# A hybrid decoder layer on one core: Toeplitz blocks read from rows of lags, rotation tables made inside the setup's loop, and a delta-net state carried by two products per chunk

## The chip, the cores and the metric

The kernel runs on one NeuronCore of a Trainium2 chip. The metric is the time of one execution on the device in microseconds; of the kernel before there are three runs and one more run under the profiler. TensorE multiplies, VectorE, ScalarE and GpSimd do the elementwise work, and DMA queues (most of them issued by SyncE) move data. The profile calls these engines PE, DVE, ACT, POOL and SP, and PEld is TensorE's loading of weights.

## The reference

One inference step of one layer: 2048 new positions, and eight single new tokens (samples) with states of their own. All is in fp32.

```python
n = rmsnorm(x, norm1_g);  proj = n @ w_in
y_s5  = s5_mixer(proj[:512], ...)          # diagonal state space, 32 groups of 16 channels, 64 states
y_gdn = gdn_mixer(proj[512:], ...)         # gated delta rule, 4 heads of 128
x = x + concat(y_s5, y_gdn) @ w_out
x = x + conv_ffn(rmsnorm(x, norm2_g))      # 1024 -> 2*2816 -> 1024, causal conv of width 3

# s5, per group: h[t] = Abar*h[t-1] + Bbar*u[t] (64 complex states),  y[t] = Re(C*h[t]) + d*u[t]

# delta rule, per head and chunk, state s (128 x 128):
decay = exp(gc_i - gc_j);  L = strict(beta * k k^T * decay)
sol   = solve(I + L, [beta*v, beta*k*exp(gc)])          # gives u_c, w_c
v_new = u_c - w_c @ s
o     = (q*exp(gc)) @ s + (q k^T * decay) @ v_new
s     = s*exp(gc_last) + (k*exp(gc_last-gc))^T @ v_new
```

The kernel takes chunks of 128 positions for the delta rule and blocks of 8 and 16 positions for the S5 scan.

## The kernel before, in words

The 2048 positions are four quarters of 512 (q = 3, 2, 1, 0 in the first loop). The large fp32 products are taken as three products of rounded halves (L287 to L289, 2992 + 928 of each), and these are most of TensorE's work. TensorE runs its instructions in one order; that order comes from the order of the steps in the program and a scheduler which plays the program through in a model of time.

**Setup (to about 240 us).** A loop over the quarters loads and normalizes x. In its third round, s5_setup makes the S5 operators, each for 8 batches of 4 groups, and writes them to DRAM: E and E2 (GpSimd, L489, three operations of 128x512 each), F and F2 (VectorE, then transposes), T2 (L510, a 128x128 product of F and E per group) and T (L516 makes one block M of 16 columns per group, L521 shifts it into 8 block columns by products with a shifted identity). T and T2 are Toeplitz: they hold one 16x16 block per lag. When the loop over batches is done its pool is closed, and a new pool s5c holds the rotation powers u0 to u10 (u[k+1] = u[k] squared, from L530) and the table CSt of all 32 groups, doubled in length six times (cmul, L337 to L342: six operations of VectorE for each complex product), which goes to tabD. The delta net's pool g is opened on the same side of SBUF when s5_setup has returned. Steps "u" (s5_in) project the S5 inputs, "c" (gdn_cols, L801 to L830) makes the delta net's gates.

**Mixers (about 240 to 620 us).** A string of letters sets the order of the steps: F gdn_front of a head (projections, conv, transposes, decay matrix; kg and vt are read from PSUM by ScalarE, L890 and L891), I gdn_inverse (the inverse T of I + L: 32x32 blocks on VectorE from an identity X copied at L924, then products), B gdn_back (four chunks in turn, L977 to L989), b and h the two halves of s5_batch, one batch of groups. s5_batch loads F, F2, tab, T, T2, E and E2 of a batch, 13 tiles in a ring (NM).

**gdn_back, a chunk.** Two products of the state (L977, L978), rv on VectorE (L980: vt minus the first, scaled), T times rv (L982), vn on VectorE, then kg times vn and AT times vn (L986, L987), and VectorE adds the state (L988) and the output (L989).

**Feed-forward (620 us to the end).** A second string does the up and down projections in pieces (r, s), and between them F, I and B of the three further quarters (12 heads). A step I is put ahead of others by a high priority.

Of the kernel before, what the change touches and what calls it, by code (L numbers as in the profile page):

```python
# [9 lines left out]
F32 = mybir.dt.float32  # L10
# [13 lines left out]
NW, NWR, NV, NG, NM, UPB = 8, 2, 9, 4, 13, 1  # L24
# [18 lines left out]
MIXERS = ("FbbhbFhhIbBbIhbhbFBIFhIhbBhxB")  # L43
FFN = ("NFIrLrrSFrrrrrrBFIrBIrrrFIrrNBFrBIrrFrBrIrrFrrIBrrFrrIBrrrrNBrFIrFrrBFIrrrrIrBBrrrrrrrrrFr"
       "rrrIBrrrrGrrrsrsrrrrrrsrsrrrrrrrr")
# [57 lines left out]
def consts(c):  # L103
# [51 lines left out]
    c.Xi = cp.tile([128, 4, 32], F32, name="Xi")  # L155
    xi = c.V("xi", I32)[:, :128].rearrange("p (a b) -> p a b", a=4)
    nc.gpsimd.iota(xi, pattern=[[-1, 4], [1, 32]], base=1024, channel_multiplier=-4)
    nc.vector.tensor_scalar(xi, xi, 31, None, op0=OP.bitwise_and)
    nc.vector.tensor_scalar(c.Xi, xi, 0.0, None, op0=OP.is_equal)
# [185 lines left out]
def s5_setup(c):  # L345

    nc, tc, inp, ps = c.nc, c.tc, c.inp, c.ps
    c.TD, c.FD, c.ED, c.TD2, c.FD2, c.ED2 = (c.dram(n, 8, 128, 512) for n in ("TD", "FD", "ED", "TD2", "FD2", "ED2"))
# [4 lines left out]
    with ExitStack() as es:  # L353
# [4 lines left out]
        def small(name, n=32):  # L358
            return sp.tile([128, n], F32, name=name)
# [22 lines left out]
        kk = small("kk")  # L382
        nc.vector.tensor_scalar(kk, th, 1.0 / (2 * math.pi), 12582912.0, op0=OP.mult, op1=OP.add)
        nc.vector.tensor_scalar(kk, kk, 12582912.0, None, op0=OP.subtract)
        r = small("r")
# [3 lines left out]
        r2, sn, cs = small("r2"), *(keep.tile([128, 32], F32, name=n) for n in ("sn", "cs"))  # L389
# [9 lines left out]
        nc.vector.tensor_scalar(cs, cs, 1.0, None, op0=OP.add)  # L399

# [14 lines left out]
        p, den, t, fr, fi = (small(n) for n in ("p_", "den", "t_", "fr", "fi"))  # L415
# [47 lines left out]
        rev = lambda P, r: P[r, :, 15::-1]  # L463
# [9 lines left out]
        AD = sp.tile([128, 32, 16], F32, name="AD", tag="Bi")  # L473
        nc.vector.tensor_tensor(AD[96:128], dbc[96:128].rearrange("p (g c) -> p g c", c=16),
                                c.ident[96:128, None, 112:128].to_broadcast([32, 32, 16]), op=OP.mult)
        shift = sp.tile([128, 240], F32, name="shift")
        nc.vector.memset(shift[:, 128:240], 0.0)
        nc.vector.tensor_copy(shift[:, 0:128], c.ident)
        for b in range(8):
            gs = slice(4 * b, 4 * b + 4)  # L480
# [3 lines left out]
            def outer(eng, dst, x, xp, y, yp):  # L484

                t = sp.tile(sh, F32, name="ot", tag="cm" if eng is nc.vector else "op", bufs=2 if eng is nc.vector else 1)
                eng.tensor_tensor(dst, x[:, gs, None, :].to_broadcast(sh), xp[:, :, :, None].to_broadcast(sh), op=OP.mult)
                eng.tensor_tensor(t, y[:, gs, None, :].to_broadcast(sh), yp[:, :, :, None].to_broadcast(sh), op=OP.mult)
                eng.tensor_tensor(dst, dst, t, op=OP.add)  # L489
            for k, dram in ((1, c.ED), (9, c.ED2)):  # L490
                E = st("Et", 2)
                outer(nc.gpsimd, E, CrT, PA[:, gs, k:k + 8], CiT, PB[:, gs, k:k + 8])
                if k == 1:
                    E1 = E
                nc.sync.dma_start(dram[b], E.rearrange("p a b c -> p (a b c)"))
# [10 lines left out]
            M = sp.tile([128, 4, 16], F32, name="M", bufs=2)  # L506

            pt = ps("s")
            for g in range(4):
                nc.tensor.matmul(pt[:, g * 128:(g + 1) * 128], lhsT=FTf[:, g], rhs=E1[:, g].rearrange("p s c -> p (s c)"), start=True, stop=True)  # L510
            T2 = sp.tile([128, 512], F32, name="T2", tag="ev", bufs=2)
            nc.scalar.activation(T2, pt, AF.Copy)
            nc.sync.dma_start(c.TD2[b], T2)
            pm = ps("s")
# [4 lines left out]
            pT = ps("s")  # L519
            for j in range(8):  # L520
                nc.tensor.matmul(pT[:, j * 64:(j + 1) * 64], lhsT=shift[:, 16 * (7 - j):16 * (7 - j) + 128],  # L521
                                 rhs=M.rearrange("p g c -> p (g c)"), start=True, stop=True)
            To = sp.tile([128, 4, 8, 16], F32, name="Tt", tag="ev", bufs=2)
            nc.scalar.activation(To, pT.rearrange("p (j g c) -> p g j c", j=8, g=4), AF.Copy)
            nc.sync.dma_start(c.TD[b], To.rearrange("p a b c -> p (a b c)"))
        inner.close()
        sp = es.enter_context(tc.tile_pool(name="s5c", bufs=1, side="right"))

        u8 = [sp.tile([128, 2, 32], F32, name=f"u{k}") for k in range(11)]
        nc.vector.tensor_copy(u8[0][:, 0], cs)  # L530
        nc.vector.tensor_copy(u8[0][lo, 1], sn[lo])
        nc.vector.tensor_scalar(u8[0][hi_, 1], sn[hi_], -1.0, None, op0=OP.mult)

        def rot(outc, outs, ac, as_, bc, bs, shape):
            cmul(nc, sp, outc, outs, ac, as_, bc, bs, shape, "rot")
        for k in range(10):
            rot(u8[k + 1][:, 0], u8[k + 1][:, 1], u8[k][:, 0], u8[k][:, 1], u8[k][:, 0], u8[k][:, 1], [128, 32])
        CSt = sp.tile([128, 2, 32, 65], F32, name="CSt")
        Ct, St = CSt[:, 0], CSt[:, 1]
        nc.vector.memset(Ct[:, :, 0], 1.0)  # L540
        nc.vector.memset(St[:, :, 0], 0.0)
        for k in range(6):
            n = 1 << k
            m = min(32, 512 // n)
            for h in range(32 // m):
                hs = slice(m * h, m * h + m)
                b_ = lambda i: u8[4 + k][:, i, hs, None].to_broadcast([128, m, n])
                rot(Ct[:, hs, n:2 * n], St[:, hs, n:2 * n], Ct[:, hs, 0:n], St[:, hs, 0:n], b_(0), b_(1), [128, m, n])
        nc.vector.tensor_copy(Ct[:, :, 64], u8[10][:, 0])
        nc.vector.tensor_copy(St[:, :, 64], u8[10][:, 1])  # L550
        for k in range(8):
            nc.sync.dma_start(c.tabD[k].rearrange("p (a r) -> p a r", a=2), CSt[:, :, 4 * k:4 * k + 4].rearrange("p a g m -> p a (g m)"))


def s5_in(c, q, nT, pre, ws, rsB):

    nc = c.nc
    for t in range(4):
        rows = slice(t * 128, t * 128 + 128)
        up = pre.tile([128, QT], F32, name="up", bufs=UPB).rearrange("p (s r m) -> p s r m", s=8, r=2)  # L560
# [915 lines left out]
```

## Time and profile before

| | |
|---|---|
| median of three runs | 2806.24 us (2805.96, 2806.24, 2814.92) |
| profiled execution | 2812.43 us, of which the span of instructions is 2810.5 us |
| PE busy | 2683.3 us, 95% of the span |
| DVE, ACT, POOL busy | 2134.0, 1388.2, 694.9 us (76%, 49%, 25%) |
| chain that ended last | PE 76%, DVE 13%, DMA 5%, ACT 2%, issue 2%, SP's queue 1% |

The chain that ended last follows back, from the last instruction, what released each step; PE holds three quarters of it. Busy shares are means over stages that differ: the setup, the mixers and the feed-forward stage are told apart by reading the busy time in stretches of the span. The granted clock stands in the same rows as a share of 2.4 GHz, so 0.50 would be a stretch wholly at 1.2 GHz.

### The profile page before, as it was taken

The numbers are of one execution on the slowest core, as the hardware profiler recorded it, in microseconds if no ns is written. First come the engines' busy times: TensorE is split into PE (matmuls) and PEld (weight loads), VectorE is DVE, ScalarE is ACT, GpSimd is POOL, SyncE is SP. The second block draws the span as 40 slices with busy tenths as digits, with TensorE's granted clock in tenths as the row PEclk, the third lists the DMA queues.
The fourth block names the chain that finished last, engine by engine and source line by source line (L and its number), as shares of the span: only waits on it lengthen the run. The fifth ranks groups of instructions, "written<-read, shape, count | busy, mean of one in ns | idle before, by whom it ended". The sixth has DMA issues, their size and how long they took to land.

```text
span 2810.5 us, 43670 instructions
## 1 busy us (share of the span) xinstructions
PE 2683.3 (95%) x15568; PEld 2290.5 (81%) x15568; DVE 2134.0 (76%) x4642; ACT 1388.2 (49%) x2774; POOL 694.9 (25%) x972
## 2 busy tenths in 40 slices
PE   5998898999999999998999999999999998999998
PEld 4887887787988999998777878877888787788887
DVE  6867887866779879778598777986777877676776
ACT  3635555555555454444544554544545445544443
POOL 4636331100121212212331111213221122322223
PEclk9999998999999999999999999999999999999999
DMA  7756443435324233333434333344333334533432
GB/s 195 240 158 189 127 131 106 123 91 152 108 83 115 84 95 87 95 92 111 130 97 117 95 91 102 89 130 125 96 103 93 92 89 128 164 98 98 129 112 68
DMA packets 427308, 325.15 MB, mean 116 GB/s; under 512 B 75823, under 2 KB 372184, under 8 KB 427075
## 3 DMA queue, kind: packets, MB, share of 16 engines
q1 hardware_dynamic: 416755, 293.76, 36.0%
q0 software_dynamic: 10336, 28.61, 3.3%
q8 instruction: 122, 2.00, 0.3%
q14 instruction: 95, 0.78, 0.1%
HBM read 268.94 MB, written 53.63 MB: 115 GB/s over the span
## 4 chain that ended last, share of the span: by engine, by line
PE 76%; DVE 13%; DMA 5%; ACT 2%; issue 2%; SPq 1%; POOL 0%; DVEq 0%; POOLq 0%; ACTq 0%
PE psmm L287 17%; PE psmm L289 17%; PE psmm L288 17%; PE psd L287 5%; PE psd L288 5%; PE psd L289 5%; DVE wlo L73 1%; DVE tm L929 1%; DMA N<-nD 1%; DVE X L930 1%; DVE x L1125 1%; DMA mr<-mixT 1%; PE psf L905 1%; PE psf L869 1%; DVE t L846 1%
## 5 line engine op out<-in xcount | busy, mean ns | idle before, releaser
L287 PE MATMUL psmm<-nT,whi 128*128 128x512 f32 (+2 forms) x2992 | 1066.8, 358 | 18.1 <-ACT t L843 5.8
L288 PE MATMUL psmm<-nT,whi 128*128 128x512 f32 (+2 forms) x2992 | 1061.8, 355 | 2.8 <-DVE nT L73 1.4
L289 PE MATMUL psmm<-nT,wlo 128*128 128x512 f32 (+2 forms) x2992 | 1060.4, 355 | 0.0
L72 ACT ACTIVATE whi<-wr 128x1024 fp32r<-128x1024 f32 x372 | 393.8, 1060 | 576.8 <-PE psmm L288 419.5
L287 PEld LDWEIGHTS psmm<-nT,whi 128*128 128x128 f32 x2992 | 570.4, 191 | 98.7 <-ACT t L843 6.8
L288 PEld LDWEIGHTS psmm<-nT,whi 128*128 128x128 f32 x2992 | 571.2, 191 | 81.1 <-DVE nT L73 3.0
L289 PEld LDWEIGHTS psmm<-nT,wlo 128*128 128x128 f32 x2992 | 570.5, 191 | 78.0 <-issue 1.1
L73 DVE TENSOR_TENSOR wlo<-wr,whi 128x1024 fp32r<-128x1024 f32 x356 | 445.0, 1251 | 96.6 <-ACT whi L72 92.7
L1125 DVE TENSOR_TENSOR x<-psd,x 128x512 f32<-128x512 f32 (+2 forms) x464 | 257.2, 558 | 134.1 <-PE psd L289 132.1
L287 PE MATMUL psd<-gt,whi 128*128 128x512 f32 (+2 forms) x928 | 324.0, 349 | 16.8 <-DVE x L1125 14.7
L288 PE MATMUL psd<-gt,whi 128*128 128x512 f32 (+2 forms) x928 | 317.2, 342 | 0.0
L289 PE MATMUL psd<-gt,wlo 128*128 128x512 f32 (+2 forms) x928 | 315.6, 341 | 0.0
L1272 DVE SCALAR_TENSOR_TENSOR t<-raw,cc,t 128x512 f32<-128x512 f32 x352 | 275.8, 785 | 15.4 <-ACT t L1269 9.7
L1273 POOL COPY halo<-raw 128x2 f32<-128x2 f32 x176 | 79.2, 450 | 778.6 <-DVE raw L1268 709.8
L287 PEld LDWEIGHTS psd<-gt,whi 128*128 128x128 f32 x928 | 175.4, 189 | 47.7 <-DVE x L1125 22.3
L73 POOL TENSOR_TENSOR gt<-s,gt 128x512 fp32r<-128x512 f32 (+1 forms) x88 | 126.2, 1434 | 333.1 <-ACT gt L72 311.5
L288 PEld LDWEIGHTS psd<-gt,whi 128*128 128x128 f32 x928 | 175.6, 189 | 21.6
L289 PEld LDWEIGHTS psd<-gt,wlo 128*128 128x128 f32 x928 | 175.1, 189 | 20.9
L1268 DVE TENSOR_TENSOR raw<-psmm,rs 128x512 f32<-128x512 f32 (+1 forms) x214 | 123.9, 579 | 71.7 <-PE psmm L289 70.3
L1269 ACT ACTIVATE t<-raw,cc 128x512 f32<-128x512 f32 (+1 forms) x176 | 127.1, 723 | 69.3 <-DVE raw L1268 66.2
L929 DVE TENSOR_TENSOR tm<-X,N 128x124 f32<-128x124 f32 (+30 forms) x496 | 131.2, 265 | 39.0 <-DMA N<-nD 27.2
L1135 POOL TENSOR_TENSOR sq<-sq 128x256 f32<-128x256 f32 (+3 forms) x84 | 96.7, 1151 | 223.8 <-ACT sq L1133 221.3
(504 smaller groups left out, 3656.1 us busy)
## 6 DMA issues: line engine op xcount, KB each, us to landing
wr<-in_ffn_w_up_dram SPq DMA_DIRECT2D x176, 512.0 KB
wr<-in_ffn_w_down_dram SPq DMA_DIRECT2D x88, 512.0 KB
wr<-in_w_in_dram SPq DMA_DIRECT2D x64, 512.0 KB
wr<-in_w_out_dram SPq DMA_DIRECT2D x32, 512.0 KB
xTD<-xT SPq DMA_DIRECT2D x32, 256.0 KB
N<-nD SPq DMA_DIRECT2D x16, 512.0 KB
mr<-mixT SPq DMA_DIRECT2D x32, 256.0 KB
xr<-xTD SPq DMA_DIRECT2D x32, 256.0 KB
```

The source lines that it names most:

```text
L72: nc.scalar.activation(hi, raw, AF.Copy)
L73: (eng or nc.vector).tensor_tensor(lo, raw, f32(hi), op=OP.subtract)
L287: nc.tensor.matmul(out, lhsT=wh, rhs=xh, start=first, stop=False)
L288: nc.tensor.matmul(out, lhsT=wh, rhs=xl, start=False, stop=False)
L289: nc.tensor.matmul(out, lhsT=wl, rhs=xh, start=False, stop=last)
L929: nc.vector.tensor_tensor(m, X[:, :, j:j + 1].to_broadcast(sh), N[:, j:j + 1, j + 1:].to_broadcast(sh), op=OP.mult)
L1125: nc.vector.tensor_tensor(x2[:, j, b0:b1], p, x2[:, j, b0:b1], op=OP.add)
L1135: c.nc.gpsimd.tensor_tensor(acc[0], acc[0], s, op=OP.add)
L1268: nc.vector.tensor_tensor(raw[:, 2 + b0:2 + b1], p, rsB[:, b0:b1], op=OP.mult)
L1269: nc.scalar.activation(t[:, :n], raw[:, 2:2 + n], AF.Copy, scale=w[2])
L1272: nc.vector.scalar_tensor_tensor(t[:, :QT], raw[:, j:j + QT], w[j], t[:, :QT], op0=OP.mult, op1=OP.add)
L1273: nc.gpsimd.tensor_copy(c.halo[:, ch], raw[:, QT:QT + 2])
```

## The change

**Toeplitz blocks.** The setup writes one row of lags per group to KD: for each of the 16 columns 23 blocks of 16, the first 7 of them zero. It makes them by products whose weights are only 16 columns wide (FTf[:, g, 0:16]), 4 x 3 per batch. s5_batch loads T and T2 of a group as one tile of 256 columns, by a DMA whose rows overlap. The inputs of a block are kept in reverse order of positions. The ring of tiles has 10 in place of 13.

**Tables.** u0 to u10 are made ahead of the loop over batches, and the table of eight groups in every second round of it, six doublings each.

**Delta net.** gdn_front makes one more tile per head, ke. After the inverse, gdn_carry multiplies ke by T for each chunk and copies the result over kq[:, 0]. A chunk of gdn_back then starts from T times vt, adds the product of the state to it in PSUM, and has vn at once. X of the inverse is loaded from DRAM. Both strings of steps differ in places.

```diff
-NW, NWR, NV, NG, NM, UPB = 8, 2, 9, 4, 13, 1
+NKE = 1
+NW, NWR, NV, NG, NM, UPB = 8, 2, 9, 4, 10, 1
-MIXERS = ("FbbhbFhhIbBbIhbhbFBIFhIhbBhxB")
+MIXERS = ("FbbhbFhhIBbbFIhbhbBFhIhbIBhxB")
...
@@ s5_setup
+        u8 = [sp.tile([128, 2, 32], F32, name=f"u{k}", tag=f"u{k if k > 3 else k % 2}") for k in range(11)]
+        def tables(i):
+            hs = slice(8 * i, 8 * i + 8)
+            CSt = sp.tile([128, 2, 8, 65], F32, name="CSt")
...
+            for k in range(6):
+                n = 1 << k
+                b_ = lambda i: u8[4 + k][:, i, hs, None].to_broadcast([128, 8, n])
+                rot(Ct[:, :, n:2 * n], St[:, :, n:2 * n], Ct[:, :, 0:n], St[:, :, 0:n], b_(0), b_(1), [128, 8, n])
...
+            for k in range(2):
+                nc.sync.dma_start(c.tabD[2 * i + k].rearrange("p (a r) -> p a r", a=2), CSt[:, :, 4 * k:4 * k + 4].rearrange("p a g m -> p a (g m)"))
-        nc.vector.tensor_copy(QA[lo], rev(PR, lo))
-        nc.vector.tensor_copy(QA[hi_], rev(PI, hi_))
-        nc.vector.tensor_scalar(QB[lo], rev(PI, lo), -1.0, None, op0=OP.mult)
-        nc.vector.tensor_copy(QB[hi_], rev(PR, hi_))
+        for W in (Wr, Wi):
+            nc.vector.tensor_scalar(W[hi_], W[hi_], -1.0, None, op0=OP.mult)
+        for k in range(10):
+            rot(u8[k + 1][:, 0], u8[k + 1][:, 1], u8[k][:, 0], u8[k][:, 1], u8[k][:, 0], u8[k][:, 1], [128, 32])
         for b in range(8):
+            if b % 2 == 0:
+                tables(b // 2)
...
-                nc.tensor.matmul(pt[:, g * 128:(g + 1) * 128], lhsT=FTf[:, g], rhs=E1[:, g].rearrange("p s c -> p (s c)"), start=True, stop=True)
-                nc.tensor.matmul(pm[:, g * 16:(g + 1) * 16], lhsT=FTf[:, g], rhs=CS[:, 4 * b + g, :], start=True, stop=True)
-            nc.vector.tensor_copy(M, pm[:, :64].rearrange("p (a b) -> p a b", a=4))
-            nc.vector.tensor_tensor(M[96:128], M[96:128], AD[96:128, gs], op=OP.add)
-            for j in range(8):
-                nc.tensor.matmul(pT[:, j * 64:(j + 1) * 64], lhsT=shift[:, 16 * (7 - j):16 * (7 - j) + 128],
+                nc.tensor.matmul(pk[:, g * 128:(g + 1) * 128], lhsT=FTf[:, g, 0:16], rhs=Es[0][:, g], start=True, stop=True)
+            nc.scalar.activation(Ka, pk, AF.Copy)
+            nc.sync.dma_start(to(1, 9), Ka.rearrange("p (g l) -> p g l", g=4))
+                nc.tensor.matmul(pk[:, g * 112:(g + 1) * 112], lhsT=FTf[:, g, 0:16], rhs=Es[1][:, g, 0:112], start=True, stop=True)
+                nc.tensor.matmul(pk[:, 448 + g * 16:464 + g * 16], lhsT=FTf[:, g, 0:16], rhs=CS[:, 4 * b + g, :], start=True, stop=True)
+            nc.scalar.activation(Ka[:, 0:448], pk[:, 0:448], AF.Copy)
+            nc.vector.tensor_tensor(Ka[:, 448:512], pk[:, 448:512], AD[:, gs].rearrange("p g c -> p (g c)"), op=OP.add)
...
-        inner.close()
-        sp = es.enter_context(tc.tile_pool(name="s5c", bufs=1, side="right"))
@@ s5_batch
-    for m, d in ((Tm, c.TD), (T2, c.TD2), (Em, c.ED), (E2, c.ED2)):
+    for g in range(4):
+        nc.sync.dma_start(T[:, g], bass.AP(tensor=c.KD.tensor, offset=c.KD.offset + (4 * t + g) * 5888, ap=[[16, 8], [368, 16], [1, 256]]))
@@ gdn_front
+    ke = gp.tile([128, 4, 128], F32, name="ke", bufs=NKE)
     for ci in range(4):
+        nc.scalar.activation(ke[:, ci], v4(pk)[:, ci], AF.Copy, scale=col[:, 6, ci, h:h + 1])
@@ gdn_inverse
-    nc.vector.tensor_copy(X, c.Xi)
+    dma(X.rearrange("p r i -> p (r i)"), c.XiD)
+def gdn_carry(c, F):
+    kq, T, ke = F[0], F[6], F[7]
+    p = c.ps("i")
+    for ci in range(4):
+        c.nc.tensor.matmul(p[:, ci * 128:(ci + 1) * 128], lhsT=ke[:, ci], rhs=T[:, ci], start=True, stop=True)
+    c.nc.scalar.activation(kq[:, 0, :QT], p, AF.Copy)
@@ gdn_back
-        pV = c.ps("b")
-        nc.tensor.matmul(pV[:, 0:128], lhsT=kq[:, 0, sl], rhs=S0, start=True, stop=True)
-        nc.vector.scalar_tensor_tensor(rv, pV[:, 0:128], col[:, 6, ci, h:h + 1], vt[:, ci], op0=OP.mult, op1=OP.add)
-        nc.tensor.matmul(pV[:, 256:384], lhsT=T[:, ci], rhs=rv, start=True, stop=True)
+        p = c.ps("b")
+        nc.tensor.matmul(p[:, 0:128], lhsT=T[:, ci], rhs=vt[:, ci], start=True, stop=False)
+        nc.tensor.matmul(p[:, 0:128], lhsT=kq[:, 0, sl], rhs=S0, start=False, stop=True)
@@ tile_hymba_step_kernel, step "I"
-                    gdn_inverse(c, h, F[-1])
+                    gdn_inverse(c, h, F[6])
+                    gdn_carry(c, F)
```

The first place is VectorE where gdn_cols of the first quarter runs. Before, its rows (ab, sxa, smx, from a PSUM bank psf) stand among the rows of the last doublings of the table CSt; u is the rotation power and cm a temporary of the complex product:

```order
L801 COPY ab<-psf 8x16
L802 COPY ab<-psf 128x64
L342 TENSOR_TENSOR CSt<-CSt,cm_1538 128x32x8
L338 TENSOR_TENSOR CSt<-CSt,u_1424 128x32x16
L341 TENSOR_TENSOR CSt<-CSt,u_1424 128x32x16
L805 TENSOR_TENSOR ab<-ab 128x5x8
L337 TENSOR_TENSOR cm_1545<-CSt,u_1424 128x512
L340 TENSOR_TENSOR cm_1546<-CSt,u_1424 128x512
L809 TENSOR_TENSOR sxa<-ab,dtb 128x20
```

In the changed kernel the same rows (numbered three lines earlier) stand behind one another, ahead of a row of the samples (ssd) and of the conv (t):

```order
L798 COPY ab<-psf 8x16
L799 COPY ab<-psf 128x64
L802 TENSOR_TENSOR ab<-ab 128x5x8
L806 TENSOR_TENSOR sxa<-ab,dtb 128x20
L807 TENSOR_SCALAR smx<-sxa 128x20
L808 SCALAR_TENSOR_TENSOR sta<-smx,sxa 128x20
L1036 TENSOR_TENSOR ssd<-ident,col 8x32
L811 TENSOR_TENSOR sta<-sta,smx 128x20
L812 TENSOR_TENSOR col<-sta,alog 128x20
```

The rows of the table have moved out of this place, ahead into the loop over batches. The second place is TensorE in a chunk of the first head's gdn_back. Before, from the product of rv to the state's products of the next chunk; the pss rows between are s5_batch's:

```order
L982 MATMUL psb<-rv,LT 128x128
L691 MATMUL pss<-hw,E_3666 128x4x32
L685 MATMUL pss<-U,Tm 128x256
L687 MATMUL pss<-U,T_3664 128x4x32
L690 MATMUL pss<-hh,Em 128x4x32
L691 MATMUL pss<-hw,Em 128x4x32
L690 MATMUL pss<-hh,E_3666 128x4x32
L691 MATMUL pss<-hw,E_3666 128x4x32
L986 MATMUL psb<-vn,kg 128x128
L987 MATMUL psb<-vn,AT 128x128
L977 MATMUL psb<-Sst,kq 128x128
L978 MATMUL psb<-Sst,kq 128x128
```

In the changed kernel, a whole chunk and the start of the next:

```order
L985 MATMUL psb<-vt,LT 128x128
L986 MATMUL psb<-Sst,kq 128x128
L987 MATMUL psb<-Sst,kq 128x128
L682 MATMUL pss<-U,T 128x256
L684 MATMUL pss<-U,T 128x4x32
L991 MATMUL psb<-vn,kg 128x128
L992 MATMUL psb<-vn,AT 128x128
L985 MATMUL psb<-vt,LT 128x128
L986 MATMUL psb<-Sst,kq 128x128
L987 MATMUL psb<-Sst,kq 128x128
```

The product with T now stands ahead of the state's products, and between these and the products of vn there is one gap, filled by two products of s5_batch. The third place is ScalarE behind the first carry, with kq<-psi the copy of gdn_carry, and the rows of the next head's front behind it:

```order
L973 ACTIVATE kq<-psi 128x512
L890 ACTIVATE ke<-psf,col 128x128
L888 ACTIVATE kg<-psf,hc 128x128
L890 ACTIVATE ke<-psf,col 128x128
L888 ACTIVATE kg<-psf,hc 128x128
```

Before, no row like the first two kinds is on this engine. Over the whole program, TensorE issues 64 products psi<-LT,ke (gdn_carry) and 32 each of the three 16-column kinds more, and 64 shifts, 32 products of T2 and 32 of M fewer; ScalarE 64 ke and 16 kq copies more; VectorE 64 rv fewer, and 102 rows of the table more.

## Rows read from the trace of the kernel before

**Rows 1.** Busy time by stretch: PE, PEld, DVE, ACT, POOL, clock, DMA share, GB/s
```profile
20.00:200.00 180.00, 161.84 (x974) 140.33 (x974) 134.95 (x288) 85.92 (x188) 82.72 (x76) 0.94 0.62 201
200.00:240.00 40.00, 28.35 (x210) 26.99 (x211) 33.50 (x113) 14.81 (x39) 22.36 (x14) 0.87 0.67 183
240.00:620.00 380.00, 346.84 (x2479) 307.81 (x2479) 293.13 (x904) 215.25 (x586) 101.44 (x144) 0.91 0.44 124
620.00:2810.00 2190.00, 2142.95 (x11897) 1813.18 (x11895) 1667.57 (x3321) 1064.50 (x1949) 474.91 (x714) 0.99 0.36 105
```

**Rows 2.** Chain of waits, 0 to 250 us: start, duration, what
```profile
187.05 4.19 DMA TD<-Tt
191.75 2.02 DVE u L530
231.22 8.00 DMA tabD<-CSt
239.64 1.22 DVE kq L856 x2
```

**Rows 3.** Timeline of 217 to 229 us: start, duration, engine, line
```profile
217.41 10.70 POOL L847 COPY gh<-raw 128x3 f32<-128x3 f32 x1
226.91 0.61 PE L818 MATMUL psf<-col,tri 128*128 128x16 f32 x2 [6.77 <-DVE col L815]
228.31 0.64 ACT L78 ACTIVATE s<-t 128x520 f32<-128x520 f32 x1 [5.53 <-POOL t L849]
```

**Rows 4.** Chain of waits, 60 to 130 us, products of the setup loop
```profile
83.61 0.89 PE pss L510 x8
86.80 0.80 PE pss L516 x8
127.11 1.73 PE pss L521 x16
```

**Rows 5.** Timeline of PE from 310 us, products with 16-column weights
```profile
310.05 0.20 PE L703 MATMUL pss<-Us,Tm 32*16 32x8 f32 x2
310.18 0.21 PE L704 MATMUL pss<-h,Em 128*16 128x8 f32 x2
```

**Rows 6.** Timeline of DVE from 205 us, two rounds of the rotation
```profile
205.07 0.19 DVE L338 TENSOR_TENSOR u<-u 128x32 f32<-128x32 f32 x1
206.38 0.20 DVE L337 TENSOR_TENSOR cm<-CSt,u 128x32 f32<-128x32 f32 x1
```

**Rows 7.** Timeline of 84 to 87 us, POOL and DVE side by side
```profile
85.61 1.29 POOL L489 TENSOR_TENSOR Et<-Et,ot 128x512 f32<-128x512 f32 x1
85.70 1.22 DVE L89 TENSOR_SCALAR rs_t<-rs_t 128x4 f32<-128x4 f32 x1
86.95 0.16 DVE L90 TENSOR_TENSOR rs_y<-rs_y,rs_t 128x4 f32<-128x4 f32 x1
```

**Rows 8.** Timeline of PE from 602 us, two products of a chunk
```profile
602.22 0.38 PE L986 MATMUL psb<-vn,kg 128*128 128x128 f32 x2
602.44 0.39 PE L987 MATMUL psb<-vn,AT 128*128 128x128 f32 x2
```

**Rows 9.** Groups of instructions: busy, mean ns, idle before and its releasers
```profile
L977 PE MATMUL psb<-Sst,kq 128*128 128x128 f32 x128 | 27.6, 298 | 9.6 <-DVE ot L989 8.7 <-DVE zs L1003 0.8
L982 PE MATMUL psb<-rv,LT 128*128 128x128 f32 x128 | 26.5, 290 | 4.7 <-ACT ot L981 4.7
L980 DVE SCALAR_TENSOR_TENSOR rv<-psb,col,vt 128x128 f32<-128x128 f32 x64 | 22.1, 345 | 19.8 <-PE psb L978 19.4
L890 ACT ACTIVATE kg<-psf,hc 128x128 f32<-128x128 f32 x64 | 18.5, 392 | 0.0
L504 ACT ACTIVATE Fi<-pss 128x512 f32<-128x512 f32 x16 | 9.6, 597 | 14.7 <-PE pss L503 11.1 <-DMA TD<-Tt 3.5
```

**Rows 10.** Timeline of PE from 364 us, one chunk
```profile
364.55 0.39 PE L978 MATMUL psb<-Sst,kq 128*128 128x128 f32 x2
370.00 0.39 PE L982 MATMUL psb<-rv,LT 128*128 128x128 f32 x2
```

More of the change, by code (lines that the diff above doesn't have):

```diff
@@ L347, in s5_setup @@
     nc, tc, inp, ps = c.nc, c.tc, c.inp, c.ps
-    c.TD, c.FD, c.ED, c.TD2, c.FD2, c.ED2 = (c.dram(n, 8, 128, 512) for n in ("TD", "FD", "ED", "TD2", "FD2", "ED2"))
+    c.FD, c.ED, c.FD2, c.ED2 = (c.dram(n, 8, 128, 512) for n in ("FD", "ED", "FD2", "ED2"))
+    c.KD = c.dram("KD", 32, 16, 23, 16)
     c.tabD = c.dram("tabD", 8, 128, 520)
@@ L356, in s5_setup, with small @@
         sp = inner.enter_context(tc.tile_pool(name="s5b", bufs=1, side="right"))
-        def small(name, n=32):
-            return sp.tile([128, n], F32, name=name)
+        def small(name, n=32, tag=None):
+            return sp.tile([128, n], F32, name=name, tag=tag or name)
         def dup_T(ap, name):
@@ L388, in s5_setup @@
         nc.vector.scalar_tensor_tensor(r, kk, -3.019915981956753e-7, r, op0=OP.mult, op1=OP.add)
-        r2, sn, cs = small("r2"), *(keep.tile([128, 32], F32, name=n) for n in ("sn", "cs"))
+        r2, sn, cs = small("r2", tag="t3"), *(keep.tile([128, 32], F32, name=n) for n in ("sn", "cs"))
         nc.vector.tensor_tensor(r2, r, r, op=OP.mult)
@@ L413, in s5_setup @@
         nc.vector.tensor_copy(c.ab1[64:128, 1], PI[64:128, :, 1])
-        p, den, t, fr, fi = (small(n) for n in ("p_", "den", "t_", "fr", "fi"))
+        p, den, t, fr, fi = (small(n, tag=g) for n, g in (("p_", "t1"), ("den", "t2"), ("t_", "t3"), ("fr", None), ("fi", None)))
         nc.vector.tensor_scalar(p, PR[:, :, 1], -1.0, None, op0=OP.add)
@@ L472, in s5_setup @@
         dbc = c.bcast("dbc", inp["s5_d"], 512, sp, tag="cm", bufs=2)
[L473 to L478, printed above, removed]
+        AD = sp.tile([128, 32, 16], F32, name="AD", tag="Bi")[0:16]
+        nc.vector.tensor_tensor(AD, dbc[0:16].rearrange("p (g c) -> p g c", c=16), c.ident[0:16, None, 0:16].to_broadcast([16, 32, 16]), op=OP.mult)
+        zero = sp.tile([128, 512], F32, name="zero", tag="cm", bufs=2)[:, :112]
+        nc.vector.memset(zero, 0.0)
+        for k in range(4):
+            nc.sync.dma_start(c.KD[8 * k:8 * k + 8, :, 0:7].rearrange("g c l d -> (g c) (l d)"), zero)
+        for k in range(10):
+            rot(u8[k + 1][:, 0], u8[k + 1][:, 1], u8[k][:, 0], u8[k][:, 1], u8[k][:, 0], u8[k][:, 1], [128, 32])
         for b in range(8):
+            if b % 2 == 0:
+                tables(b // 2)
             gs = slice(4 * b, 4 * b + 4)
@@ L538, in s5_setup @@
[L538 to L548, printed above, removed]
@@ L634, in s5_batch @@
     mat = lambda n: sp.tile([128, 520], F32, name=n, tag="mat", bufs=NM)
-    Fm, F2, tab, Tm, T2, Em, E2 = (mat(n) for n in ("Fm", "F2", "tab", "Tm", "T2", "Em", "E2"))
+    Fm, F2, tab, Em, E2 = (mat(n) for n in ("Fm", "F2", "tab", "Em", "E2"))
+    T = sp.tile([128, 4, 256], F32, name="T", bufs=2)
     nc.sync.dma_start(F2[:, :512], c.FD2[t])
@@ L698, in s5_batch @@
         G = 4 * t + g
-        nc.tensor.matmul(p[:, 8 * g:8 * g + 8], lhsT=F[96:128, g], rhs=c.Us[96:128, G], start=True, stop=True)
+        nc.tensor.matmul(p[:, 8 * g:8 * g + 8], lhsT=F[0:32, g], rhs=c.Us[0:32, G], start=True, stop=True)
     for g in range(4):
@@ L702, in s5_batch @@
         o = p[:16, 32 + 8 * g:40 + 8 * g]
-        nc.tensor.matmul(o, lhsT=T[0:32, g, 0:16], rhs=c.Us[0:32, G], start=True, stop=False)
+        nc.tensor.matmul(o, lhsT=T[96:128, g, 0:16], rhs=c.Us[96:128, G], start=True, stop=False)
         nc.tensor.matmul(o, lhsT=E[:, g, 0:16], rhs=c.h0[:, 0, G], start=False, stop=True)
```

100 lines of the change are left out of this document (45 added, 55 removed).

## Prediction

> **What bounds the kernel now.** I read the busy shares of the page first, where PE is busy 95% of the span and the chain that ended last lies on PE for 76%. So only two things can move the time: work that PE does, and the 127 us in which it does none. The table of busy time by stretch [rows 1] shows where the idle lies: PE is busy 161.84 of 180 us in 20 to 200 (the setup), 28.35 of 40 in 200 to 240 (tables and gates), 346.84 of 380 in 240 to 620 (mixers) and 2142.95 of 2190 after that. The reader should see that the worst share is in the short second stretch, where the granted clock is also lowest (0.87 of 2.4 GHz on the mean, so part of it ran at 1.2 GHz, PE having idled in it), while the mixers hold 33.2 us of idle in all. The change touches each of these three.
>
> Next I read the chain of waits up to 250 us [rows 2]: the rotation's first row on VectorE (L530) starts at 191.75, when the last Toeplitz block has landed in DRAM (a transfer that began at 187.05 and took 4.19), and its table leaves for DRAM at 231.22, in a transfer of 8.00 that the delta net's first buffer (kq, 239.64) waits for. The timeline there [rows 3] shows who suffers: PE waits 6.77 us at L818 for the gate row col, which stood behind table rows on VectorE, and ScalarE waits 5.53 us behind GpSimd, whose copy of 128x3 took 10.70 us.
>
> All sums are against the profiled execution, 2812.4 us (span 2810.5), which is 6.2 us above the median of the runs, 2806.2; the forecast of the median is therefore the sum less 6.2.
>
> **A. Toeplitz blocks, PE's work in the setup.** Removed per batch are eight shifts that take 1.73 us from first to last (the row counts two instructions for each), four T2 products at 0.89 and four M products at 0.80 [rows 4]: 3.42 us, times 8 batches 27.4. Added are 12 products per batch with 16-column weights. Small products with such weights start 0.13 us apart [rows 5]; full 128x128 products start 0.22 apart [rows 8]. With 128 and 112 moving columns I take 0.20 each and 0.13 for the 16-column ones: 8 x 4 x (0.20 + 0.20 + 0.13) = 17.0. The balance is 10 us of PE time. PE has 18.2 us of idle in this stretch, so some of its work there is not what ends it. If VectorE or GpSimd set the pace of the loop, the gain is 0; if two evictions of PSUM also go off the path (L504, 597 ns each for 128x512 [rows 9], in all 8 fewer of them), it is 15. I take -10, nearest to the work counted, ends -15 and 0.
>
> **B. Tables out of 200 to 240.** With the rows of the table gone from between gdn_cols' rows, col follows ab without them, and the gap at L818 and part of ScalarE's go; g's memory no longer waits for the table's transfer. What can go is PE's idle of 11.65 us there plus what the low clock cost, 0.13 x 40 = 5.2: 17 at most. Some of the idle belongs to gdn_cols itself, whose rows pass between three engines. I take -11, ends -17 and 0 (0 if the stretch was only waiting for the conv's work, which stays).
>
> What the tables cost in the loop is VectorE's time. 60 rows of u at 0.11 (12 rows from 205.07 to 206.38 [rows 6]) are 6.6. The old table's 42 rows stand between 191.75 and 231.22 beside the gates and the conv; less the 6.6, half of what is left is 16, an estimate. Cutting them into 144 adds 102 x 0.11 = 11. So 34 us go to a stretch where VectorE is busy 134.95 of 180: 169. PE's own pace is its cover, at nothing, but with only 11 us to spare; if the cover is gone this is the slower rival below.
>
> One row speaks against the change here. VectorE's L89 on 128x4 elements took 1.22 us while GpSimd's L489 ran for 1.29, and the next of the same size, L90, took 0.16 when it had ended [rows 7]. The Trainium skill (SBUF — State Buffer, section Who interferes with whom) has a rule for it: an instruction of VectorE with two inputs in SBUF and one of GpSimd that reads SBUF lock each other out for a whole instruction. The trace agrees in kind, 1.22 against 0.16; all 144 rows of the table have two inputs in SBUF, and by the rule each of them can be caught, which would give the slower rival's time in place of mine.
>
> **C. The carry, PE's work.** gdn_back has as many products as before (T times rv becomes T times vt), and gdn_carry adds four per head: 64, at 0.22 from start to start [rows 8], is 14.1 us. Where they fall in idle time they cost nothing: they stand in PE's queue behind the inverse's last small products, where it waits anyway. But PE is busy 98% of the stretch in which 12 of the 16 heads lie [rows 1], so I take +12, ends +5 and +15.
>
> **D. A shorter chunk.** The step by VectorE between the state's products and T's goes (L980, 64 of 345 ns, 22.1 us [rows 9]). In one chunk of the mixers the state's product stands at 364.55 and T's at 370.00 [rows 10], 5.45 us for what is now no step at all; mostly PE fills this with s5_batch or projections. What is late next is vn, which waits for the state's products in the same way. PE's waits before the back's products are 9.6 us at L977 and 4.7 at L982 [rows 9]: 14.3. L982's hop vanishes, L977's (for the state from the head before, and for a free bank) stays in part. I take half, -7, ends -14 and 0.
>
> **E. What waits for the carry.** The carry's copy over kq[:, 0] is one of 128x512 on ScalarE (0.60 us, by L504 [rows 9]). The next head's ke and kg (392 ns each [rows 9]) stand behind it on that engine, since ke has one buffer that the carry must have read; they hold the PSUM bank of that head's transposes, and behind these PE's queue holds the next front's products. So a head whose inverse ends late now holds the next front. 16 carries at 0 to 0.75 us: 0 to +12. I take +4. 64 more ke evictions (64 x 0.39 = 25 us) are hidden by ScalarE's idle, half of the span.
>
> X by DMA in place of a copy, the reversed order of inputs, the four loads of T (the bytes of two tiles of 128x512, as before) and the ring of 10 tiles in place of 13 I put at 0: the DMA share is 0.44 in the mixers [rows 1]. If a batch's loads come late for want of a buffer, the mixers lose up to a few us, which the range holds.
>
> **Sum.** -10 - 11 + 12 - 7 + 4 = -12: 2812.4 - 12 = 2800.4 in a profile, and 2794 for the median. With all good ends it is -15 - 17 + 5 - 14 + 0 = -41, with all bad ones 0 + 0 + 15 + 0 + 12 = +27; both at once are unlikely, and this outcome's own range is 2781 to 2807.
>
> **The rivals.**
>
> *R1, slower: VectorE and GpSimd lock each other in the setup loop.* GpSimd is busy 82.72 of the 180 us [rows 1], a share of 0.46. A table row caught behind an instruction of 1.29 us waits 0.65 on the mean: 144 x 0.46 x 0.65 = 43 us. VectorE would then need 169 + 43 = 212 where the stretch has 180: +32; if half of the rows run in GpSimd's gaps, 190 and +10. I price it at +20; A's 10 then is no gain. +20 - 11 + 12 - 7 + 4 = +18: 2824. It decides from the point where VectorE's busy time in 20 to 200 passes some 175 us. For it speaks L89, against it that VectorE idles 45 us there now, and that the scheduler can place table rows beside PE's projections when GpSimd has nothing.
>
> *R2, much faster: the back's chain limits the mixers.* PE idles 33.2 us in 240 to 620, with a clock of 0.91. If the chain of chunks over heads is what ends that stretch, a hop of up to 5.45 us less in 16 chunks lets nearly all of the idle go: D is -30. -10 - 11 + 12 - 30 + 4 = -35: 2771. For it speaks that four heads run their chunks one after another in this stretch; against it that the waits put down to the back's products are only 14.3 us in the whole span.
>
> *R3, nothing gained.* The hops are places in PE's queue and not waits, the freed 10 us of PE in the setup are taken up by waiting for VectorE, and the stretch 200 to 240 keeps its length because the conv of the first front sets it. A 0, B -6, C +12, D 0, E 0, and the string's new order gives or takes a few: +6 at most, -6 at least, so 2800 to 2812, centre 2806. For it speaks that many changes off PE's path vanish at 95% busy.
>
> **How the numbers follow.** The forecast has 0.42, R1 0.18, R2 0.18, R3 0.22. A measurement of this kernel tells about 0.3%, 8.4 us, from no change. The forecast lies 12 below; with its own range three quarters of it (0.31) are faster by over that and a quarter (0.11) within. R2 is faster (0.18); R3 is within (0.22); R1 is slower, but for a part near its lower end (0.01 within). So faster 0.49, within 0.34, slower 0.17. The range goes from R2's centre, 2770, to 2820, which leaves out half of R2 below and R1's upper half above.
>
> **What would show it.** A: in the new profile PE's busy time of the setup stretch falls by some 10 us and the end of the loop comes earlier by as much; if VectorE's busy share there is above 97%, R1 holds. B: no wait of some 7 us before the first gate product of gdn_cols, and a granted clock above 0.87 after the setup. C: 64 new products on psi from ke, some 0.22 apart. D: the 4.7 us of waiting before T's product is gone, and the mixers stretch is shorter by up to 10 us; if it is shorter by 25 or more, R2 holds. E: waits of PE put down to ke, kg or kq, some 4 us in all; if they are above 12, C and E together eat all that is gained. My prediction is wrong if the mixers or the feed-forward stage change by more than 20 us, as neither holds a term of that size.

## The result, and the profile after

The changed kernel takes 2846.38 us (the median of four runs, 2844.08 to 2848.0) beside 2809.84 us of the kernel before: 1.0132 times as long, 95% interval 1.0116 to 1.0147. That is some 37 us slower, where 12 us faster was forecast. The profiled execution took 2848.0 us with a span of 2846.2.

Two rows cut both kernels at nearly the same work: ScalarE's second exponential of the first gates, and VectorE's scaling of the first up projection of the feed-forward stage. In before:

```profile
231.40 0.18 ACT L824 ACTIVATE col<-psf 128x16 f32<-128x16 f32 x1
804.76 0.43 DVE L1268 TENSOR_TENSOR raw<-psmm,rs 128x256 f32<-128x256 f32 x1
```

After:

```profile
236.31 0.18 ACT L821 ACTIVATE col<-psf 128x16 f32<-128x16 f32 x1
836.88 0.43 DVE L1273 TENSOR_TENSOR raw<-psmm,rs 128x256 f32<-128x256 f32 x1
```

Busy time up to and between them, columns as in [rows 1], first of before, then of after:

```profile
0.00:231.40 231.40, 184.94 (x1136) 160.87 (x1137) 168.36 (x405) 102.31 (x229) 116.12 (x111) 0.94 0.64 195
231.40:804.80 573.40, 531.00 (x3614) 466.85 (x3614) 427.91 (x1258) 321.80 (x818) 120.38 (x168) 0.93 0.45 124
```

```profile
0.00:236.30 236.30, 174.87 (x1031) 138.08 (x1032) 178.11 (x505) 97.90 (x220) 102.94 (x106) 0.92 0.60 174
236.30:836.90 600.60, 547.41 (x3698) 481.83 (x3697) 426.20 (x1228) 335.93 (x859) 124.34 (x173) 0.93 0.45 121
```

The setup ends 4.9 us later although PE works 10.1 us less in it: its idle grew from 46.5 to 61.4. The mixers take 27.2 us more, 16.4 of them PE busy and 10.8 idle; what follows takes about 4 more. By the fixed stretches that answer to [rows 1]:

```profile
20.00:200.00 180.00, 137.81 (x738) 104.00 (x738) 162.98 (x464) 82.66 (x185) 76.48 (x73) 0.90 0.56 179
200.00:240.00 40.00, 38.62 (x318) 36.37 (x317) 13.07 (x31) 13.95 (x37) 13.95 (x11) 1.00 0.53 136
240.00:620.00 380.00, 339.76 (x2415) 304.72 (x2414) 279.49 (x858) 210.18 (x567) 105.07 (x143) 0.90 0.46 125
```

The hole of 200 to 240 is closed: PE idles 1.4 us there in place of 11.65, at the full 2.4 GHz. But 24 us of new idle stand in 20 to 200 (42.2 in place of 18.2), with VectorE busy for 163 us, and PE waits for VectorE there:

```profile
PE pss L527 <- DVE FTs L513: 9.7, 3, 7.0
PE psf L216 <- DVE nT L225: 8.8, 4, 3.9
PE psmm L288 <- DVE up L561: 8.5, 3, 4.0
PE psmm L289 <- DVE nT L225: 4.9, 3, 2.4
```

(Waits of PE in 20 to 200 after the change: us in all, times, longest.) The S5 inputs are late from the first on. The first VectorE row that scales them stands at 44.95 before, at 58.44 after (timeline of VectorE, before and after):

```profile
44.95 1.00 DVE L567 TENSOR_TENSOR up<-psmm,rsB 128x512 f32<-128x512 f32 x1
```

```profile
58.44 1.01 DVE L561 TENSOR_TENSOR up<-psmm,rsB 128x512 f32<-128x512 f32 x1 [1.07 <-ACT rsB L242]
```

The tables' edit is not its cause: the setup's part alone (e_setup below), which has it too, has that row at 46.8. The delta net's rows that answer to [rows 9] (groups of instructions of after):

```profile
L991 PE MATMUL psb<-vn,kg 128*128 128x128 f32 x128 | 28.1, 302 | 10.4 <-ACT ot L990 10.3
L985 PE MATMUL psb<-vt,LT 128*128 128x128 f32 x128 | 27.1, 295 | 5.5 <-DVE ot L994 4.7 <-DVE zs L1008 0.6
L986 PE MATMUL psb<-Sst,kq 128*128 128x128 f32 x128 | 26.1, 287 | 1.9 <-ACT kq L973 1.9
L972 PE MATMUL psi<-LT,ke 128*128 128x128 f32 x128 | 17.1, 276 | 0.5 <-ACT LT L964 0.5
```

Of before, one more row belongs beside L977 and L982 of [rows 9]:

```profile
L986 PE MATMUL psb<-vn,kg 128*128 128x128 f32 x128 | 26.8, 292 | 1.6 <-DVE vn L984 1.5
```

So PE waited 15.9 us at the chunk's products before (9.6, 4.7 and 1.6); now it waits 17.8 at L991, L985 and L986. L991's wait is put down to ScalarE's copy ot, which reads another part of the PSUM tile that L991 writes. Before, that product wrote a tile of its own, though the two tiles took turns in the one buffer that both kernels give to this use (b=1 in PB).

### The profile page after: what moved, and what is told of

It reads as the page before. It is cut to its first block, busy times and chain, and to the rows that moved or that the text cites. A ratio compares the mean times of both kernels' runs of the same rounds, so it can differ in the third digit from the quotient of the medians.

```text
span 2846.2 us, 44041 instructions
## 1 busy us (share of the span) xinstructions
PE 2695.9 (95%) x15632; PEld 2290.2 (80%) x15632; DVE 2124.2 (75%) x4665; ACT 1411.4 (50%) x2854; POOL 688.1 (24%) x972
## 4 chain that ended last, share of the span: by engine, by line
PE 74%; DVE 13%; DMA 7%; ACT 3%; issue 2%; SPq 1%; POOL 1%; POOLq 0%; DVEq 0%; ACTq 0%
PE psmm L288 17%; PE psmm L289 16%; PE psmm L290 16%; PE psd L288 5%; PE psd L289 5%; PE psd L290 5%; DVE wlo L74 1%; DVE tm L928 1%; DMA N<-nD 1%; DVE X L929 1%; DVE x L1130 1%; DMA mr<-mixT 1%; PE psf L904 1%; DMA wr<-in_ffn_w_down_dram 1%; ACT whi L73 1%
## 5 line engine op out<-in xcount | busy, mean ns | idle before, releaser
L74 DVE TENSOR_TENSOR wlo<-wr,whi 128x1024 fp32r<-128x1024 f32 x356 | 439.3, 1234 | 121.7 <-ACT whi L73 111.3
```

The costliest lines, as they stand in the source:

```text
L74: (eng or nc.vector).tensor_tensor(lo, raw, f32(hi), op=OP.subtract)
```

## The experiments

All are compared with the kernel before, run on the same chip. "Over before" is the ratio less one, times 2810 us. Two versions are set side by side by these ratios; where their intervals overlap, the difference between them is not shown. Theory 1 was that the setup and the mixers lose separately; when the first four runs contradicted it, a theory on the edit of X took its place.

| version | ratio to before, 95% interval | over before |
|---|---|---|
| changed kernel | 1.0132 (1.0116 to 1.0147) | +37 |
| e_setup | 1.0015 (1.0005 to 1.0025) | +4 |
| e_toep | 1.0028 (1.0013 to 1.0043) | +8 |
| e_gdn | 1.0073 (1.0058 to 1.0088) | +21 |
| e_gdn_oldstr | 1.0060 (1.0045 to 1.0075) | +17 |
| e_xonly | 1.0073 (1.0050 to 1.0097) | +21 |
| e_xonly_late | 1.0042 (1.0026 to 1.0059) | +12 |
| e_xonly_gate | 1.0042 (1.0028 to 1.0056) | +12 |
| e_gdn_xlate | 1.0095 (1.0069 to 1.0120) | +27 |
| e_after_oldstr | 1.0081 (1.0058 to 1.0104) | +23 |
| e_after_xlate | 1.0072 (1.0044 to 1.0099) | +20 |
| e_after_gate | 1.0114 (1.0096 to 1.0131) | +32 |
| e_after_xlate_gate | 1.0073 (1.0056 to 1.0090) | +21 |
| e_after_nox8_gate | 1.0057 (1.0041 to 1.0073) | +16 |
| e_gdn_nox8_gate | 1.0054 (1.0034 to 1.0073) | +15 |
| e_carry2 | 1.0090 (1.0069 to 1.0110) | +25 |
| e_carry0 | 1.0028 (1.0015 to 1.0040) | +8 |
| e_toep_gate | 0.9989 (0.9975 to 1.0004) | -3 |
| e_setup_gate | 1.0024 (1.0010 to 1.0037) | +7 |

**Each part alone.** The edits are the hunks of the diff, by function; the ring stays at 13 tiles where the Toeplitz blocks stay as before.

> The delta net's part alone (ke, gdn_carry, the new chunk, X from DRAM, both new strings), with the setup, the tables and the 13 tiles of before. Theory 1 (two separate losses, one in the setup loop and one in the mixers): +15 to +22 us over before, with the setup ending where it did before. Theory 2 (all of the loss comes from VectorE's table rows in the setup loop, and the mixers only start from a worse place): within 6 us of before. Theory 3 (the mixers lose all of it): +30 or more.

> The delta net's part alone, but with both strings of steps as before. If the order of the steps in the new strings costs the time, this is 10 us or more faster than the same kernel with the new strings. If the strings were needed for the carry, it is slower than that. If neither, the two are within 5 us.

> The setup's part alone (Toeplitz blocks from rows of lags, tables in the loop, ring of 10), with the delta net and strings of before. Theory 1: +12 to +22 us, nearly all of it before the first gate row. Theory 2: +30 or more. Theory 3: within 6 us of before, or faster, since A and B pay for what the loop loses.

> The Toeplitz blocks alone, with the tables after the loop as before and the delta net of before. By my sum's term A: -10 (0 to -15) against before. If the loss of the setup lies in the table rows, this is faster than before or the same, and the setup with both edits is 15 us or more slower than this. If the rows of lags themselves cost time (narrow products, loads of T, ring of 10), this is slower than before by 5 or more.

The setup's part costs only 4 us; the delta net's costs 21, and the two together 37, not 25. In e_gdn the first S5 row was late too (60.5), with the setup of before. So the late start comes with the delta net's edits, and of these only X adds anything ahead of the first head. The old strings were 4 us faster here: within the intervals.

The Toeplitz blocks alone, at +8 where A said -10, missed too, though not in the setup: in e_toep the gate row stands at 211.10, 20 us earlier than before. The inverse of its third head is long, with rows of the next quarter's normalization in it (42.6 us against 29.4); what that costs is taken up below.

**X alone, and its write moved.**

```diff
 e_xonly (before, with:)
-    c.Xi = cp.tile([128, 4, 32], F32, name="Xi")
+    xi, Xi = (c.V(n, t)[:, :128].rearrange("p (a b) -> p a b", a=4) for n, t in (("xi", I32), ("Xi", F32)))
...
+    nc.sync.dma_start(c.XiD, Xi.rearrange("p a b -> p (a b)"))
...
-    nc.vector.tensor_copy(X, c.Xi)
+    dma(X.rearrange("p r i -> p (r i)"), c.XiD)
 e_after_xlate, e_gdn_xlate, e_xonly_late: the making of Xi and its write
+                make_X(c)     # after the loop over quarters, ahead of PRE
             st.n = nTs[0]
```

> The kernel before with one edit: X of the inverse is written once to DRAM in the constants' part and loaded by DMA per head, in place of the copy on VectorE. Theory X (the one write of X stands in SP's queue ahead of the stores of x, waits there for two VectorE rows that come late, and so delays the weights, the scales and the first inputs): the first split of u comes 8 to 15 us later than before and the time is +4 to +15. Rival (the loads of X or the mixers' order cost, not the write): the first u is at its place of before; the loss lies after 240 us. Second rival: it costs nothing (within 3 us).

> The changed kernel with X and its one write to DRAM made after the setup instead of among the constants; all else as changed. Theory X: the setup's 28 us of lateness go for the greater part, and the time falls by 10 to 22 us against the changed kernel, to some +15 to +27 over before. Rival (the loop of the setup is bound by VectorE's table rows whatever the start): within 5 us of the changed kernel.

> The delta net's part alone with the write of X after the setup. Theory X: 4 to 10 us faster than the delta net's part as it is, and what is left over before (10 to 16 us) is the carry's 64 products (8 to 14 us). If the carry's copy and ke cost waits of their own, what is left is above 18.

> The changed kernel with both strings of steps as before. In the delta net's part alone the old strings were 3 us faster; the same here (0 to -6 against the changed kernel) if the strings are a cost of their own, +5 or more if the new order belongs to the other edits.

> The kernel before with X loaded from DRAM per head, but written there after the setup. X from DRAM with the early write was +20 over before. If the early write in SP's queue is the cause, within 5 us of before, with the first split of u at its place. If the loads per head and the place they give to the inverse are the cause, +10 or more with a start as before.

The edit on X, which I had put at 0, costs 21 us alone. The same row of e_xonly, and of e_xonly_late:

```profile
59.67 1.00 DVE L567 TENSOR_TENSOR up<-psmm,rsB 128x512 f32<-128x512 f32 x1
```

```profile
43.96 1.00 DVE L572 TENSOR_TENSOR up<-psmm,rsB 128x512 f32<-128x512 f32 x1
```

So the early part of the edit makes the start late: the two VectorE rows that make X, their place among the shared buffers (c.V; before, X had a buffer of its own) and the write. The runs move the three together and don't say which it is. The write's own wait doesn't explain it: in SP's queue of e_xonly it goes out at 23.79 and the store of x behind it at 24.22, against 22.73 before. What differs is the order of all that follows. In e_xonly the S5 operators come earlier and the inputs later: GpSimd's first row of E stands at 45.77 in place of 50.51, and the scales of the inputs are written at 57.20 in place of 43.87. The rows of E, of before and then of e_xonly:

```profile
50.51 2.52 POOL L487 TENSOR_TENSOR Et<-CTre,PA 128x512 f32<-128x512 f32 x2 [6.86 <-DVE PA L460]
45.77 4.16 POOL L487 TENSOR_TENSOR Et<-CTre,PA 128x512 f32<-128x512 f32 x2
```

In e_xonly this exchange is nearly paid back: its ninth S5 row is 1.4 us late and its gate row 5 (236.42). In e_xonly_late the start is as before and yet the gate row stands at 244.99, so the 9 us between the two versions, whose intervals overlap, aren't won in the setup, and 12 are left without a late start. In the changed kernel the move brings the gate row from 236.31 to 225.93 and gives 17 us, the intervals apart. e_gdn_xlate went against theory X: with its first S5 row at 43.76 it was no faster than e_gdn (the intervals overlap). So moving the early part is shown to give time only where the tables are in the loop as well. The old strings gave 14 us in the changed kernel where at most 6 were expected.

**The rest of X's cost: the third head's inverse.** An inverse is a chain of 62 small VectorE rows. In e_xonly, as in the changed kernel, the eight normalizations of the next quarter (nrm, nT) stand among those of the third head; in before none does. Timeline of VectorE in e_xonly:

```profile
463.16 0.18 DVE L930 TENSOR_TENSOR X<-X,tm 128x20 f32<-128x20 f32 x1
463.26 0.69 DVE L660 TENSOR_TENSOR hh<-hh,Xw 128x512 f32<-128x512 f32 x1
463.86 0.68 DVE L73 TENSOR_TENSOR nT<-nrm,nT 128x512 fp32r<-128x512 f32 x1
464.46 0.74 DVE L195 SCALAR_TENSOR_TENSOR nrm<-xT,cc,rsB 128x512 f32<-128x512 f32 x1
465.12 0.17 DVE L929 TENSOR_TENSOR tm<-X,N 128x16 f32<-128x16 f32 x1
```

From X's first row to its last the third head takes 29.4 us before (425.5 to 454.9), 50.5 in e_xonly, 45.3 in the changed kernel, 30.4 in e_setup. Busy time in 440 to 580 of before and of e_xonly, columns as above:

```profile
440.00:580.00 140.00, 129.31 (x853) 109.15 (x851) 108.56 (x388) 75.94 (x211) 18.42 (x30) 0.89 0.40 104
```

```profile
440.00:580.00 140.00, 121.16 (x741) 100.90 (x742) 97.87 (x344) 69.18 (x197) 20.67 (x32) 0.82 0.38 96
```

PE ran 112 fewer instructions in the same stretch, idled 8 us more and had a lower granted clock (0.82 of 2.4 GHz on the mean, so more of it at 1.2). The added wait ("gate") keeps those rows out:

```diff
     rsB = c.V("rsB")[:, :QT]
+    if q == 1:
+        nc.sync.dma_start(rsB[:, :128], bass.AP(tensor=c.xD[0].tensor, offset=c.xD[0].offset, ap=[[128, 128], [1, 128]]))
```

> The kernel before with X loaded from DRAM, and one added wait: the scales that the next quarter's normalization reads are loaded only when the third head's X has been stored, so that no row of that normalization can stand among the 62 VectorE rows of that head's inverse (eight of them stand there with X from DRAM alone, none in the kernel before). Theory N (what X from DRAM costs is this place: the inverse of the third head grows from 29 to 50 us and TensorE runs out of work): 9 to 16 us faster than X from DRAM alone, at +3 to +10 over before. Rival (the early write in SP's queue, or the loads of X, cost it): within 4 us of X from DRAM alone.

> The changed kernel with the same added wait. Theory N: 9 to 16 us faster than the changed kernel (2846), at +20 to +28 over before; what is left is the setup's lateness of some 14 and the carry's products of some 6 to 9. Rival: within 4 us of the changed kernel.

> The changed kernel with the write of X after the setup and the added wait: both suspected places mended. If the two are separate and add up: 2846 less 17 (the late write) less 9 to 16 (the wait), so 2813 to 2822, +5 to +13 over before, which is the carry's 64 products. If the late write had already taken the same microseconds as the wait does: 2826 or more.

> The changed kernel without its edit on X (X copied on VectorE as before, from a constant of one byte per element so that it fits in SBUF; two small tiles have one buffer in place of two), and with the added wait. Nothing of X's write or loads is left. If X was the cause of the lost start, this is within 5 us of the version with the late write and the wait; if another edit of the delta net delays the start, the first split of u is late here too (by 8 us or more against before) and the time is 10 us or more above it.

Theory N was that the long third inverse is what X costs. The wait shortens it to 34.3 us in e_xonly and to 33.0 in the changed kernel; it gives 9 us and 5, less than the 9 to 16 expected in the second, and the intervals overlap in both. With the late write it shortens the inverse from 45.4 to 29.2 us and gives nothing, so the inverse's length alone isn't the price. With the wait in both, leaving out X's edit takes the changed kernel from 32 over before to 16, the intervals apart: that is what X costs there (two small tiles also have one buffer less in the version without it).

**The carry.** Both start from e_after_nox8_gate:

```diff
 e_carry2
-    for ci in range(4):
+    for ci in (0, 1, 2, 3, 0, 1, 2, 3):
         c.nc.tensor.matmul(p[:, ci * 128:(ci + 1) * 128], lhsT=ke[:, ci], rhs=T[:, ci], ...)
 e_carry0: these products and the copy over kq[:, 0] left out
```

> The changed kernel without its edit on X and with the added wait (2826 in its runs), with each product of the carry done twice into the same PSUM, one after the other: 64 more products, no other instruction. If TensorE's time is what the carry costs (term C, 64 x 0.22), +10 to +15 over that version. If the carry stands where TensorE waits anyway, +0 to +4, and what is left over before has another cause.

> The same version with the carry's 64 products and its 16 copies left out (the chunk then reads k in place of the carried factor, so the delta net's outputs differ from the reference; all else is computed). If C and E hold, 12 to 20 us faster than the same version with the carry, at about before's time or the setup part's (2809 to 2815). If the rest lies in the new chunk itself or in the 64 ke rows, it stays at 2820 or more.

> The delta net's part alone, without its edit on X (X from a constant of one byte per element) and with the added wait; setup and tables as before. If the carry's products are the cost and the shorter chunk gives nothing, +10 to +16 over before. If the shorter chunk gives back what term D says, +3 to +8. If the mixers of the changed kernel lose by what the setup does to them, within 4 us of before.

Doubling the 64 products costs 9 us (the intervals just overlap), taking them away with their copies gives 8, less than the 12 to 20 expected: the carry is worth some 8 to 9 us, by an estimate 0.14 us for a product that takes 0.22 in the queue (in the trace of the changed kernel the eight halves of a carry start within 0.8 us). The delta net's part without X is 15 over before, and the setup's edits add nothing clear to it here (16).

**The setup's two halves with the wait.**

> The Toeplitz blocks alone with the added wait. Theory N (normalization rows among the inverse's rows cost the mixers): 4 to 9 us faster than the Toeplitz blocks alone, at -3 to +4 against before; if term A's 10 us arrived as a whole, -6 or lower. Rival: no change against the Toeplitz blocks alone (+8).

> The setup's part alone with the added wait. No normalization row stands in the third head's inverse in either, so by theory N the wait gives nothing and costs little: within 4 us of the setup's part alone (+4 over before). If it is more than 5 us slower, the wait itself has a price that the other versions paid too.

The Toeplitz blocks alone reach 0.9989, the best version of the study, but 1 lies in the interval. The wait gives them 11 us, the intervals apart, and their third inverse goes from 42.6 to 33.0: the clearest case for theory N. With the tables in the loop as well it is 1.0024: the tables cost some 10 us there (the intervals of the two do not meet, 1.0010 to 1.0037 and 0.9975 to 1.0004). Without the wait that cost doesn't show: e_setup is at 1.0015 and e_toep at 1.0028, and the intervals overlap.

## Why the prediction was wrong

**Two steps failed.** The first is the one on X: "X by DMA in place of a copy ... I put at 0". I priced X by the copy it saves and the bytes it moves, and not by the order that a scheduler gives to all that stands around its early rows and around the inverse. It cost 21 us alone, and 16 in the changed kernel with the wait. The second is that what leaves PE in the setup comes off the time while VectorE takes up the tables "at nothing": A and B were to give 21 us, and together they cost 4 alone (e_setup), 7 with the wait and 1 on top of the delta net. By the versions, the 37 us are 21 that go when X's edit is left out and the wait put in, 1 for the setup's part and 15 for the delta net's, where the forecast had 0, -21 and +9. So the second miss is as large as the first, and without X's edit the kernel (2826) would still lie outside the 2770 to 2820 of the forecast. The prediction's own sign of being wrong came as well: the mixers grew by 27.2 us. Within X's 21, what is the order of the start and what the inverse isn't separated: 17 went where only the making and the write were moved, 5 where only the wait was added, and the two do not add.

**A, -10.** Right as PE's work, mis-sized as time: the rows that A replaces were busy 34.8 us (16.8, 9.5 and 8.5 at L521, L510 and L516) and take 25.1 now (9.5, 9.1 and 6.5 at L535, L540 and L541). Yet the Toeplitz blocks give -3 (-7 to +1) at the end, with the wait, though they bring the gate row forward by 20 us. Where the rest of those 20 is lost wasn't settled.

**B, -11.** The hole closed, but moving the tables wasn't needed for most of it: in e_toep, with the tables still after the loop, their last row ends at 201.2 in place of 228.1, and PE idles 4.7 us in the same stretch where before idled 11.65:

```profile
200.00:240.00 40.00, 35.30 (x275) 34.77 (x273) 18.61 (x40) 21.24 (x60) 11.27 (x19) 0.91 0.79 219
```

That the tables' rows would be hidden was wrong: with them in the loop the gate row stands 8 us later (219.38 in e_setup, 211.10 in e_toep), and at the end they cost some 10 us with the wait. Their 144 rows took 52.3 us of VectorE, 24 of each of six lines at means of 433, 418, 400, 374, 311 and 243 ns, where I had counted 27. Timeline of the changed kernel:

```profile
73.47 1.13 POOL L512 TENSOR_TENSOR ot<-CTim,PB 128x512 f32<-128x512 f32 x1
73.69 1.06 DVE L339 TENSOR_TENSOR CSt<-CSt,u 128x128 f32<-128x128 f32 x1
74.67 0.28 DVE L342 TENSOR_TENSOR CSt<-CSt,u 128x128 f32<-128x128 f32 x1
74.67 1.40 POOL L513 TENSOR_TENSOR Et<-Et,ot 128x512 f32<-128x512 f32 x1
74.87 1.35 DVE L338 TENSOR_TENSOR cm<-CSt,u 128x128 f32<-128x128 f32 x1
76.15 0.28 DVE L341 TENSOR_TENSOR cm<-CSt,u 128x128 f32<-128x128 f32 x1
```

A row of 128x128 takes 0.28 us, but 1.06 and 1.35 where GpSimd runs a row, and ends 0.15 us behind it. The Trainium skill (SBUF — State Buffer, section Who interferes with whom) has them lock each other out for a whole instruction; the trace agrees. The row that the prediction took for this, L89, was not a case of two inputs (it is a TENSOR_SCALAR with one); the row ahead of it in the kernel before is one, ending when GpSimd's L487 does (85.65):

```profile
84.65 1.02 DVE L88 TENSOR_TENSOR rs_t<-rs_t,rs_a 128x4 f32<-128x4 f32 x1
```

So R1's mechanism is there and so is its sign, at a smaller price: VectorE's busy time reached 163 to 167 us in 20 to 200, not the 175 from which I let it decide. That it makes the late start grow (13.5 us at the first S5 row, 28 at the ninth, where e_xonly without the tables' rows recovers to 1.4) fits the traces, but no run shows it by itself. R1's terms for the setup, +20 and -11, come nearest to the +1 to +7 measured. R3's terms as listed add up to +6 and not to the 0 at which it was centred.

**C, +12.** The sign is right and the size within its ends; it measures 8 to 9.

**D, -7.** No gain is to be seen: PE's waits at the chunk's products went from 15.9 to 17.8 us, at other products. The prediction said that vn would wait for the state's products in the same way, and yet took half of the waiting as gained. Before, ScalarE's read of ot held T times rv (4.7 us at L982, [rows 9]); now it stands, with vn, between the state's products and kg times vn, and holds that (10.4 at L991). The Trainium skill (PSUM — Partial Sum Buffer, section PSUM bank collisions raise a hardware error) says that no two engines may be on one bank of a partition at once; the waits at L982 before and L991 after agree with programs that keep them apart. A version in which kg times vn writes another bank wasn't run.

**E, +4.** Not separated: e_carry0 takes away the copies too and gives no more than the products that e_carry2 doubles, so the copies cost little; of PE's waits in the changed kernel 1.9 us are put down to kq (L986), where some 4 to ke, kg or kq were expected. Without the carry 8 us are left (e_carry0), about the setup's own 4 to 7; no further cause is shown, as each figure is uncertain by about 4. The strings' new order, which the forecast's sum left out and R3 put at 6 us at most, was 14 us slower than the old in the changed kernel (1.0132 against 1.0081, the intervals apart) and 4 in e_gdn. The trace fits theory N there: with the old strings no normalization stands in the third head's inverse, which takes 26.7 us in place of 45.3. No run shows that this is the whole of the 14.

## What to carry to other kernels

An edit that neither computes nor moves anything worth a microsecond can cost more than any that was priced when a scheduler re-plans around it: price every new instruction by its place, and read both orders around the longest dependent chains before pricing its duration. Work removed from the busiest engine need not come off the time (here 10 us of work removed gave 3 us, with 0 in the interval), and work moved into a loop is hidden only if the engine that feeds the loop has slack. And test the parts alone: here they did not add (4 and 21 made 37).

## What the runs showed of the hardware

The small VectorE rows beside GpSimd's (0.28 against 1.06 and 1.35 us) were expected in kind. Not expected was how far executions of one program spread: e_toep ran from 2809.44 to 2826.77 us, so a difference of 10 us between two versions needs several runs of each.
